# A two-layer trunk kernel: the first loads in two transfers, the third block's load behind the first cast, the last norm weight ahead of the factor

## The chip, the cores and the metric

The kernel runs on one core of one Trainium2 chip. The metric is the device time of one execution in microseconds, lower is better. The core has five engines with their own instruction streams: TensorE (PE, matmuls; PEld is its weight load), VectorE (DVE), ScalarE (ACT), GpSimd (POOL) and SyncE (SP), which here only issues transfers. ACT and POOL issue a few transfers too. Data move between DRAM, on-chip memory (128 partitions) and PSUM, where matmuls accumulate.

## What is computed

The reference is a decoder trunk with 256 positions of width 1024, in float32, with two layers. Each layer is an attention, a SwiGLU feed-forward and a gated per-layer input; a root-mean-square norm stands before each of them and at the end.

```python
def reference(x, p, ...):
    h = x
    for i in range(DEPTH):                                 # DEPTH = 2
        u = _rmsnorm(h, attn_norm_g[i])
        if i % N_MIXERS == 0:                              # layer 0: forgetting attention
            proj = u @ fox_w_in[j]                         # 1024 x (3 * 1024 + 16)
            ...
            h = h + _merge_heads(_fox_attention(q, k, v, log_f)) @ fox_w_o[j]
        else:                                              # layer 1: block-sparse attention, position bias
            ...
            h = h + _merge_heads(_moba_attention(q, k, v, rel_bias_table)) @ moba_w_o[j]
        u = _rmsnorm(h, ffn_norm_g[i])
        gu = u @ ffn_w_in[i]                               # 1024 x 5632
        h = h + (jax.nn.silu(gu[..., :D_FF]) * gu[..., D_FF:]) @ ffn_w_out[i]
        gate = jax.nn.sigmoid(_rmsnorm(h, ple_norm_g[i]) @ ple_w_gate[i])
        h = h + gate * (p[i] @ ple_w_up[i])
    return _rmsnorm(h, final_norm_g)
```

## The kernel before

**Three products for one.** Each float32 operand is split into a rounded part and a remainder (`hi`, `lo`), and each product is the sum of three matmuls (`mm3`, L94 to L96): hi by hi, hi by lo, lo by hi. So each weight tile is fetched from DRAM into a `raw` tile (128 x 1024, 512 KB, six buffers), rounded by ScalarE into `whi` (L169, for some tiles L139 or L187) and subtracted by VectorE into `wlo` (L171, L142, L188). 216 such tiles go through in the order of use. SP issues the fetches one after another (L154, L138, L186). A fetch waits until VectorE has freed its buffer, and everything behind it on SP waits with it. Each transfer also takes the next of eight completion semaphores in turn and waits until the transfer eight before it has landed.

**The start.** TensorE first runs `WARM` = 8 matmuls on constants (L114, tile `cold`). The first product is v = norm(x) by the value weights. x comes transposed, in eight blocks of 128 x 256, and goes with the weight row of the same number. ScalarE scales a block by the norm's gains into `g` (`Norm.block`, L207), VectorE makes its remainder (L209). Block 0 and the gains come in tile `gx`, its weights in `raw` by halves: one half of the weights and the second half of x on SP, the gains with the first half of x and the other half of the weights on ACT. Blocks 1 and 2 come with their weight rows from the array `wx` into tile `hw` (L151), block 1 in two transfers, block 2 in one. Then come the weights of block 3, the rest of x (L295), constants (`con`, L302) and more weight tiles. The first half of each of the first three casts is VectorE's (L162), the others are ScalarE's.

**Order.** A scheduler sets the order of each engine's instructions. `tc.issue_after(x)` keeps what is issued inside it behind x on x's engine. `state["row"]` is set at every fetch of L154 and names the latest.

**The position bias of layer 1.** In layer 0, after the third pair of heads, a table is computed and written to DRAM (`d`, L429). Four transfers spread it from DRAM to DRAM (`d_0` to `d_3`, L434, 768 KB each); they are called in the feed-forward of layer 0, behind the weight fetch of that moment (L816, L817). Layer 1 loads the spread bias (L440).

**Turned probabilities.** The attention of layer 0 turns its probabilities through DRAM: POOL writes `dt` (L655) and reads it back as `pt` (L659), in part also from SP; TensorE takes `pt` in L674 and L676 (`po`).

**The end.** The last layer's gate goes token by token in two halves of 128 tokens. For the last 128 tokens and the last 512 columns, `part` takes 256 columns at a time: a sigmoid (L913), two VectorE steps (L914, L916) and a sum of squares (L959). POOL makes the norm factor from it (L962, `colf`). Then ScalarE scales the first 512 columns (L988), and VectorE scales the last two pieces of 256 by the factor and the norm weight `gb` in one step (L991). `rows` stores each piece (L966).

Of the kernel before, what the change touches and what calls it, by code (L numbers as in the profile page):

```python
# [30 lines left out]
ALU = mybir.AluOpType  # L31

P = 128
# [15 lines left out]
NCHUNK = 54  # L49
WARM = 8  # L50
RAW = 6
# [18 lines left out]

GX = 64 + S
CON = 9 * LINE
# [3 lines left out]
def trunk(ctx: ExitStack, tc: tile.TileContext, xg, wx, xr, pt, w, cst, gf, rel, hot, rvm, out):  # L76
# [47 lines left out]
    hx = [gx[:, GX - S:], hw[:, 0, 0:S], hw[:, 1, 0:S]] + [hr[:, k] for k in range(KT - 3)]  # L124

    state = {"next": 0}

    def half(at=0, entry=0):


        i = state["next"]
        state["next"] += 1
        if i not in (1, 2):
            raw = work.tile([P, HW + LINE], F32, tag="raw", bufs=RAW, name=f"raw{i}")
        ht, lt = (work.tile([P, HW + 2 * LINE], F32R, tag=n, bufs=6, name=f"{n}{i}") for n in ("whi", "wlo"))
        hi, lo = ht[:, at:at + HW], lt[:, at:at + HW]
        if entry:
            nc.sync.dma_start(raw[:, 0:HW], w[i - 2][:, 0:HW])  # L138
            nc.scalar.activation(hi, raw[:, 0:HW], AF.Copy)  # L139
            ats = [(at + FURTHER, 0, entry), (at + LINE, entry, HW)]  # L140
            for a, c0, c1 in ats:
                nc.vector.tensor_tensor(lt[:, a + c0:a + c1], raw[:, c0:c1], f32(hi[:, c0:c1]), op=ALU.subtract)  # L142
            return hi, [lt[:, a + k * P:a + (k + 1) * P] for a, c0, c1 in ats for k in range(c0 // P, c1 // P)]
        if i in (1, 2):
            raw = hw[:, i - 1, S:]
        parts = 2 if i < 2 else 1
        cs = [slice(q * HW // parts, (q + 1) * HW // parts) for q in range(parts)]
        for c in cs:
            if i in (1, 2):
                at = slice(c.start + (S if c.start else 0), c.stop + S)  # L150
                nc.sync.dma_start(hw[:, i - 1, at], wx[i - 1][:, at])  # L151
            else:
                queue = nc.scalar if i == 0 and c.start else nc.sync
                state["row"] = queue.dma_start(raw[:, c], w[max(i - 2, 0)][:, c])  # L154
# [5 lines left out]
        for c in cs:  # L160
            if i < 3 and c.start == 0:
                nc.vector.tensor_copy(hi[:, c], raw[:, c])  # L162
                with tc.issue_after(state["hi0"].ins) if i else nullcontext():
                    got, low = nm.block(i, hx[i], 1 if i else 2)
            elif i == 0:
                with tc.issue_after(got.ins):
                    state["hi0"] = nc.scalar.activation(hi[:, c], raw[:, c], AF.Copy)
            else:
                state["hi"] = state[f"hi{i}"] = nc.scalar.activation(hi[:, c], raw[:, c], AF.Copy)  # L169
            with tc.issue_after(low.ins) if i == 0 else nullcontext():  # L170
                nc.vector.tensor_tensor(lo[:, c], raw[:, c], f32(hi[:, c]), op=ALU.subtract)  # L171
        return hi, lo
# [6 lines left out]
    def gapped(first=0):  # L179
# [5 lines left out]
        ht, lt = (work.tile([P, HW + 2 * LINE], F32R, tag=n, bufs=6, name=f"{n}{i}")[:, at] for n in ("whi", "wlo"))  # L185
        nc.sync.dma_start(raw[:, 0:WW], w[i - 2])  # L186
        nc.scalar.activation(ht, raw[:, 0:WW], AF.Copy)  # L187
# [677 lines left out]
    def ple(layer, nm, ut, nx):  # L865
# [88 lines left out]
        def part(i, bk):  # L954
            c0 = HC + i * S
            first = gate(bk, 1, c0, c0 + S)
            sq = work.tile([P, HC], F32, tag="t2k", bufs=3, name=f"sql{i}")
            hc = summed(1, c0, c0 + S)
            nc.vector.tensor_tensor_reduce(sq[:, 0:S].rearrange("p (m x) -> p m x", m=4), hc, hc, 1.0 / D, ms[:, 1, i:i + 1], op0=ALU.mult, op1=ALU.add,  # L959
                                           accum_out=ms[:, 1, i + 1:i + 2])  # L960
            if i == 1:
                nc.gpsimd.tensor_tensor(col[:, 1:2], ms[:, 1, 2:3], nhalf[:, 0:1], op=ALU.pow)  # L962
            return first
# [19 lines left out]
        for c0 in (0, HC):  # L983
# [3 lines left out]
            rows(0, c0, c0 + HC, nc.sync)  # L987
        nc.scalar.activation(ys[:, 1, 0:HC], ys[:, 1, 0:HC], AF.Copy, scale=col[:, 1:2])  # L988
        rows(1, 0, HC, nc.scalar)
        for c in (slice(HC, HC + S), slice(HC + S, D)):  # L990
            nc.vector.scalar_tensor_tensor(ys[:, 1, c], ys[:, 1, c], col[:, 1:2], gb[:, c], op0=ALU.mult, op1=ALU.mult)  # L991
            rows(1, c.start, c.stop, nc.sync)

# [134 lines left out]
```

## Time and profile before

| | |
|---|---|
| time, median of 3 runs | 634.96 us (634.74 to 635.93) |
| the profiled execution, its own time | 634.63 us |
| its span in the profile | 632.8 us |
| PE busy | 624.2 us, 99% |
| PEld busy | 602.8 us, 95% |
| DVE busy | 467.7 us, 74% |
| ACT busy | 384.7 us, 61% |
| POOL busy | 43.4 us, 7% |
| moved | 135.27 MB, 214 GB/s over the span |

The profile is that of one execution; the span runs from its first instruction to its last. A row of the timeline has the start, the length, the engine, the line of the kernel, the operation, out<-in, the shape and the number of instructions merged, and in brackets the idle time before it with what ended it. A row of issued transfers has the number, the size of one and the median us from its issue to its landing. SPq, ACTq and POOLq are the issues of transfers on an engine. Buffer numbers are left out of names. A sum over the whole span says little about either end of it.

### The profile page before, as it was taken

The numbers are of one execution on the slowest core, as the hardware profiler recorded it, in microseconds if no ns is written. First come the engines' busy times: TensorE is split into PE (matmuls) and PEld (weight loads), VectorE is DVE, ScalarE is ACT, GpSimd is POOL, SyncE is SP. The second block draws the span as 40 slices with busy tenths as digits, with TensorE's granted clock in tenths as the row PEclk, the third lists the DMA queues.
The fourth block names the chain that finished last, engine by engine and source line by source line (L and its number), as shares of the span: only waits on it lengthen the run. The fifth ranks groups of instructions, "written<-read, shape, count | busy, mean of one in ns | idle before, by whom it ended". The sixth has DMA issues, their size and how long they took to land.

```text
span 632.8 us, 13104 instructions
## 1 busy us (share of the span) xinstructions
PE 624.2 (99%) x5241; PEld 602.8 (95%) x5241; DVE 467.7 (74%) x757; ACT 384.7 (61%) x663; POOL 43.4 (7%) x85
## 2 busy tenths in 40 slices
PE   9999999999999999999999999999999999999995
PEld 6899989999999999999989998999999999999984
DVE  6888888886666666668894898979666666666695
ACT  6668887754444445448774798768444444454653
POOL 0103340000000000000000044100000000000001
PEclk9999999999999999999999999999999999999998
DMA  8767878398766666666574698855766666665622
GB/s 336 259 192 236 252 241 314 120 351 259 244 206 197 199 193 208 193 208 180 191 239 171 205 295 232 296 197 180 256 199 186 195 197 202 200 208 180 197 50 85
DMA packets 41885, 135.27 MB, mean 214 GB/s; under 512 B 5248, under 2 KB 10848, under 8 KB 41824
## 3 DMA queue, kind: packets, MB, share of 16 engines
q1 hardware_dynamic: 37616, 124.11, 60.8%
q0 software_dynamic: 3488, 9.44, 5.1%
q10 hardware_dynamic: 720, 0.89, 0.4%
q8 instruction: 41, 0.67, 0.4%
q14 instruction: 20, 0.16, 0.1%
HBM read 126.01 MB, written 8.15 MB: 212 GB/s over the span
## 4 chain that ended last, share of the span: by engine, by line
PE 92%; DVE 3%; DMA 1%; issue 1%; SPq 1%; ACT 0%; POOL 0%; POOLq 0%; DVEq 0%; ACTq 0%
PE gu L95 13%; PE gu L94 13%; PE gu L96 13%; PE fo L96 6%; PE fo L95 6%; PE fo L94 6%; PE pq L94 5%; PE pq L96 5%; PE pq L95 4%; PE wo L94 2%; PE wo L95 2%; PE wo L96 2%; PE v L94 2%; PE v L95 2%; PE v L96 2%; PE v L456 1%
## 5 line engine op out<-in xcount | busy, mean ns | idle before, releaser
L171 DVE TENSOR_TENSOR wlo<-raw,whi 128x1024 fp32r<-128x1024 f32 (+1 forms) x168 | 203.5, 1216 | 65.1 <-ACT whi L169 64.8
L169 ACT ACTIVATE whi<-raw 128x1024 fp32r<-128x1024 f32 x166 | 173.7, 1056 | 94.4 <-issue 42.5
L95 PE MATMUL gu<-g,whi 128*128 128x256 f32 x704 | 194.7, 277 | 0.0
L94 PE MATMUL gu<-g,whi 128*128 128x256 f32 x704 | 194.6, 276 | 0.0
L96 PE MATMUL gu<-g,wlo 128*128 128x256 f32 x704 | 194.5, 276 | 0.0
L96 PEld LDWEIGHTS gu<-g,wlo 128*128 128x128 f32 x704 | 132.3, 188 | 0.0
L95 PEld LDWEIGHTS gu<-g,whi 128*128 128x128 f32 x704 | 132.2, 188 | 0.1
L94 PEld LDWEIGHTS gu<-g,whi 128*128 128x128 f32 x704 | 132.2, 188 | 0.0
L96 PE MATMUL fo<-fp,wlo 128*128 128x256 f32 x352 | 97.3, 276 | 0.0
L95 PE MATMUL fo<-fp,whi 128*128 128x256 f32 x352 | 97.2, 276 | 0.0
L94 PE MATMUL fo<-fp,whi 128*128 128x256 f32 x352 | 97.2, 276 | 0.0
L94 PE MATMUL pq<-g,whi 128*128 128x256 f32 x256 | 71.5, 279 | 0.0
L96 PE MATMUL pq<-g,wlo 128*128 128x256 f32 x256 | 70.9, 277 | 0.1
L95 PE MATMUL pq<-g,whi 128*128 128x256 f32 x256 | 70.8, 277 | 0.0
L188 DVE TENSOR_TENSOR wlo<-raw,whi 128x1080 fp32r<-128x1080 f32 x36 | 46.1, 1282 | 29.9 <-ACT whi L187 29.9
L94 PEld LDWEIGHTS fo<-fp,whi 128*128 128x128 f32 x352 | 66.1, 188 | 0.0
L95 PEld LDWEIGHTS fo<-fp,whi 128*128 128x128 f32 x352 | 66.1, 188 | 0.0
L96 PEld LDWEIGHTS fo<-fp,wlo 128*128 128x128 f32 x352 | 66.1, 188 | 0.0
L187 ACT ACTIVATE whi<-raw 128x1080 fp32r<-128x1080 f32 x36 | 39.6, 1101 | 28.6 <-PE gu L95 27.1
L94 PEld LDWEIGHTS pq<-g,whi 128*128 128x128 f32 x256 | 48.1, 188 | 1.0 <-issue 0.3
L96 PEld LDWEIGHTS pq<-g,wlo 128*128 128x128 f32 x256 | 48.2, 188 | 0.3 <-DVE wlo L171 0.3
L95 PEld LDWEIGHTS pq<-g,whi 128*128 128x128 f32 x256 | 48.1, 188 | 0.1
(194 smaller groups left out, 1038.8 us busy)
## 6 DMA issues: line engine op xcount, KB each, us to landing
raw<-w SPq DMA_DIRECT2D x177, 512.0 KB, 4.4
raw<-w SPq DMA_DIRECT2D x36, 540.0 KB, 4.3
dt<-turn POOLq DMA_DIRECT2D x10, 384.0 KB, 3.4
pt<-dt POOLq DMA_DIRECT2D x40, 96.0 KB, 5.2
d<-d SPq DMA_DIRECT2D x4, 768.0 KB, 7.1
bias<-d SPq DMA_DIRECT2D x4, 512.0 KB, 7.7
pt<-turn POOLq DMA_DIRECT2D x16, 96.0 KB, 3.1
pt<-turn SPq DMA_DIRECT2D x8, 96.0 KB, 3.3
```

The lines of the kernel that those rows point to most:

```text
L94: mm(o, ah, bh, start=start, stop=False, skip_group_check=True)
L95: mm(o, ah, bl, start=False, stop=False, skip_group_check=True)
L96: return mm(o, al, bh, start=False, stop=stop, skip_group_check=True)
L169: state["hi"] = state[f"hi{i}"] = nc.scalar.activation(hi[:, c], raw[:, c], AF.Copy)
L171: nc.vector.tensor_tensor(lo[:, c], raw[:, c], f32(hi[:, c]), op=ALU.subtract)
L187: nc.scalar.activation(ht, raw[:, 0:WW], AF.Copy)
L188: state["lo"] = nc.vector.tensor_tensor(lt, raw[:, 0:WW], f32(ht), op=ALU.subtract)
L456: got = mm(bks[2 * t + hf], x[a][:, t * P:(t + 1) * P], w[b][:, hf * HC:(hf + 1) * HC], start=k + a + b == 0, stop=k + b == KT, skip_group ...
```

## The change

Block 0 now comes whole in tile `gx`, which is widened by 1024 columns: first half of the weights, 64 columns of gains, x, second half of the weights. Two transfers on SP bring it (L121, L122), cut in the middle of x; ACT issues none. Behind the first cast VectorE copies one element per partition into the tile that block 2's transfer writes (L162), so that this transfer waits for the cast, and what stands behind it on SP waits too. `WARM` is 7. `state["row"]` is set once, at the second of the two transfers; the four spreading transfers of the bias name it still.

At the end, `part` multiplies its 256 columns by the norm weight after the sum of squares. The last step only scales: ScalarE 384 columns, VectorE 2 x 320.

```diff
-WARM = 8
+WARM = 7
...
-GX = 64 + S
+GX = 64 + S + HW
...
-    nc.scalar.dma_start(gx[:, 0:GX - P], xg[:, 0:GX - P])
-    gn = gx[:, 0:7 * KT].rearrange("p (n k) -> p n k", k=KT)
+    sides = gx[:, 0:HC], gx[:, GX - HC:]
+    nc.sync.dma_start(gx[:, 0:HC + 64 + P], xg[:, 0:HC + 64 + P])
+    state = {"next": 0, "row": nc.sync.dma_start(gx[:, HC + 64 + P:], xg[:, HC + 64 + P:])}
+    gn = gx[:, HC:HC + 7 * KT].rearrange("p (n k) -> p n k", k=KT)
...
-                queue = nc.scalar if i == 0 and c.start else nc.sync
-                state["row"] = queue.dma_start(raw[:, c], w[max(i - 2, 0)][:, c])
-                if i + c.start == 0:
-                    nc.sync.dma_start(gx[:, GX - P:], xg[:, GX - P:])
+            elif i:
+                nc.sync.dma_start(raw[:, c], w[i - 3][:, c])
...
-                nc.vector.tensor_copy(hi[:, c], raw[:, c])
+                nc.vector.tensor_copy(hi[:, c], part)
+                if i == 0:
+                    nc.vector.tensor_copy(hw[:, 1, 0:1], gx[:, 0:1])
...
+            gc = gb[:, HC:].rearrange("p (m a x) -> p m (a x)", m=4, x=32)[:, :, i * 2 * 32:(i + 1) * 2 * 32]
+            nc.vector.tensor_tensor(hc, hc, gc, op=ALU.mult)
             if i == 1:
                 nc.gpsimd.tensor_tensor(col[:, 1:2], ms[:, 1, 2:3], nhalf[:, 0:1], op=ALU.pow)
...
-        nc.scalar.activation(ys[:, 1, 0:HC], ys[:, 1, 0:HC], AF.Copy, scale=col[:, 1:2])
-        rows(1, 0, HC, nc.scalar)
-        for c in (slice(HC, HC + S), slice(HC + S, D)):
-            nc.vector.scalar_tensor_tensor(ys[:, 1, c], ys[:, 1, c], col[:, 1:2], gb[:, c], op0=ALU.mult, op1=ALU.mult)
-            rows(1, c.start, c.stop, nc.sync)
+        cut = 3 * P
+        nc.scalar.activation(ys[:, 1, 0:cut], ys[:, 1, 0:cut], AF.Copy, scale=col[:, 1:2])
+        rows(1, 0, cut, nc.scalar)
+        for c0, c1 in ((cut, 704), (704, D)):
+            nc.vector.tensor_scalar(ys[:, 1, c0:c1], ys[:, 1, c0:c1], col[:, 1:2], None, op0=ALU.mult)
+            rows(1, c0, c1, nc.sync)
```

The lines that build the arrays on the host follow the new layout and are left out.

Three places in the order of instructions. First SP at the program's start, before the change; the brackets name the engines and transfer semaphores (DMAHW) that a row waits for.

```order
L154 DMA raw_87<-w 128x512
L156 DMA gx<-xg 128x128
L151 DMA hw<-wx 128x768
L151 DMA hw<-wx 128x512
L151 DMA hw<-wx 128x1280
L154 DMA raw_119<-w 128x1024
L295 DMA hw<-xr 128x1280 [waits DMAHW0_49]
L302 DMA con<-cst 128x576 [waits DMAHW1_49]
```

SP at the same place after the change:

```order
L121 DMA gx<-xg 128x704
L122 DMA gx<-xg 128x640
L151 DMA hw<-wx 128x768
L151 DMA hw<-wx 128x512
L151 DMA hw<-wx 128x1280 [waits DVE_49]
L153 DMA raw_116<-w 128x1024
L295 DMA hw<-xr 128x1280
L302 DMA con<-cst 128x576
```

The first two rows carry what four transfers on two queues carried, the fifth waits for VectorE, and the seventh and eighth no longer wait for an earlier landing.

Second, SP in the attention of layer 0, from the transfer that writes the table of the position bias (`d`) on; before the change:

```order
L429 DMA d_518<-rv 16x384 [waits DVE_49]
L154 DMA raw_845<-w 128x1024 [waits DMAHW6_49,DVE_49]
L186 DMA raw_999<-w 128x1080 [waits DMAHW7_49,DVE_49]
L154 DMA raw_1030<-w 128x1024 [waits DMAHW0_49,DVE_49]
L154 DMA raw_1096<-w 128x1024 [waits DMAHW1_49,DVE_49]
L154 DMA raw_1114<-w 128x1024 [waits DMAHW2_49,DVE_49]
```

The same stretch after the change:

```order
L429 DMA d_515<-rv 16x384 [waits DVE_49]
L153 DMA raw_842<-w 128x1024 [waits DMAHW4_49,DVE_49]
L434 DMA d_0_517<-d_515 128x1536 [waits DMAHW2_49]
L186 DMA raw_996<-w 128x1080 [waits DMAHW5_49,DVE_49]
L153 DMA raw_1027<-w 128x1024 [waits DMAHW6_49,DVE_49]
L434 DMA d_1_518<-d_515 128x1536 [waits DMAHW7_49]
L434 DMA d_2_519<-d_515 128x1536 [waits DMAHW0_49]
L153 DMA raw_1093<-w 128x1024 [waits DMAHW1_49,DVE_49]
L434 DMA d_3_520<-d_515 128x1536
L153 DMA raw_1111<-w 128x1024 [waits DMAHW3_49,DVE_49]
```

The four spreading transfers stood 32 rows and more behind the table's write, seven rows apart; now all four follow within eight rows of it.

Third, VectorE at the program's end, before (ISA is the sum of squares with its read-out) and after:

```order
L914 TENSOR_TENSOR pgt_1_768_7966<-pgt_1_768_7966,ut_7585 128x256 [waits Activation_49]
L916 TENSOR_TENSOR end<-ut_7585,pgt_1_768_7966 128x4x64 [waits DVE_49]
L959 ISA sql_7970,msf<-end,msf 128x256 [waits DVE_49]
L959 ISA msf 128x1
L991 SCALAR_TENSOR_TENSOR end<-end,colf 128x256 [waits Pool_49]
L991 SCALAR_TENSOR_TENSOR end<-end,colf 128x256
```

```order
L914 TENSOR_TENSOR pgt_1_768_7964<-pgt_1_768_7964,ut_7582 128x256 [waits Activation_49]
L916 TENSOR_TENSOR end<-ut_7582,pgt_1_768_7964 128x4x64 [waits DVE_49]
L959 ISA sql_7968,msf<-end,msf 128x256 [waits DVE_49]
L959 ISA msf 128x1
L962 TENSOR_TENSOR end<-end 128x4x64 [waits DVE_49]
L994 TENSOR_SCALAR end<-end,colf 128x320 [waits DVE_49,Pool_49]
L994 TENSOR_SCALAR end<-end,colf 128x320
```

The multiply by the norm weight (L962) now stands ahead of the wait for POOL's factor.

More of the change, by code (lines that the diff above doesn't have):

```diff
@@ L119, in trunk @@
     gx = one.tile([P, GX], F32, name="gx")
-    nc.scalar.dma_start(gx[:, 0:GX - P], xg[:, 0:GX - P])
-    gn = gx[:, 0:7 * KT].rearrange("p (n k) -> p n k", k=KT)
+    sides = gx[:, 0:HC], gx[:, GX - HC:]
+    nc.sync.dma_start(gx[:, 0:HC + 64 + P], xg[:, 0:HC + 64 + P])
+    state = {"next": 0, "row": nc.sync.dma_start(gx[:, HC + 64 + P:], xg[:, HC + 64 + P:])}
+    gn = gx[:, HC:HC + 7 * KT].rearrange("p (n k) -> p n k", k=KT)
     hw = work.tile([P, 3, S + HW], F32, tag="bias", bufs=1, name="hw")
     hr = hw[:, 2].rearrange("p (k s) -> p k s", s=S)
-    hx = [gx[:, GX - S:], hw[:, 0, 0:S], hw[:, 1, 0:S]] + [hr[:, k] for k in range(KT - 3)]
-    state = {"next": 0}
+    hx = [gx[:, HC + 64:HC + 64 + S], hw[:, 0, 0:S], hw[:, 1, 0:S]] + [hr[:, k] for k in range(KT - 3)]
     def half(at=0, entry=0):
@@ L132, in half @@
         state["next"] += 1
-        if i not in (1, 2):
+        if i > 2:
             raw = work.tile([P, HW + LINE], F32, tag="raw", bufs=RAW, name=f"raw{i}")
@@ L137, in half @@
         if entry:
-            nc.sync.dma_start(raw[:, 0:HW], w[i - 2][:, 0:HW])
+            nc.sync.dma_start(raw[:, 0:HW], w[i - 3][:, 0:HW])
             nc.scalar.activation(hi, raw[:, 0:HW], AF.Copy)
@@ L159, in half @@
                 table(AF.Abs_reciprocal_sqrt)
-        for c in cs:
+        for q, c in enumerate(cs):
+            part = raw[:, c] if i else sides[q]
             if i < 3 and c.start == 0:
-                nc.vector.tensor_copy(hi[:, c], raw[:, c])
+                nc.vector.tensor_copy(hi[:, c], part)
+                if i == 0:
+                    nc.vector.tensor_copy(hw[:, 1, 0:1], gx[:, 0:1])
                 with tc.issue_after(state["hi0"].ins) if i else nullcontext():
@@ L166, in half @@
                 with tc.issue_after(got.ins):
-                    state["hi0"] = nc.scalar.activation(hi[:, c], raw[:, c], AF.Copy)
+                    state["hi0"] = nc.scalar.activation(hi[:, c], part, AF.Copy)
             else:
-                state["hi"] = state[f"hi{i}"] = nc.scalar.activation(hi[:, c], raw[:, c], AF.Copy)
+                state["hi"] = state[f"hi{i}"] = nc.scalar.activation(hi[:, c], part, AF.Copy)
             with tc.issue_after(low.ins) if i == 0 else nullcontext():
-                nc.vector.tensor_tensor(lo[:, c], raw[:, c], f32(hi[:, c]), op=ALU.subtract)
+                nc.vector.tensor_tensor(lo[:, c], part, f32(hi[:, c]), op=ALU.subtract)
         return hi, lo
@@ L1107 @@
     ins = {
[L1108 removed]
+        "xg": np.concatenate([seq[0][:, :HC], np.pad(gains.reshape(P, 7 * KT), ((0, 0), (0, 64 - 7 * KT))), xt[0], seq[0][:, HC:]], axis=1),
         "wx": wx,
```

8 lines of the change are left out of this document (3 added, 5 removed).

## The prediction

> **What bounds the kernel now.** I read the page first, then the chain of work that ended last over its first 18 us, then the timeline of that stretch, the transfers issued in it, the timeline of the last 8 us, and last the transfers between 40 and 80 us.
>
> ```profile
> span 632.8 us, 13104 instructions
> PE 92%; DVE 3%; DMA 1%; issue 1%; SPq 1%; ACT 0%; POOL 0%; POOLq 0%; DVEq 0%; ACTq 0%
> ...
> 1.65 5.73 DMA hw<-wx
> ...
> 7.97 8.52 PE v L456 x36
> ```
>
> The first two rows are the page's: TensorE (PE) is 92% of a chain of 632.8 us. The last two stand near the head of that chain: a transfer issued at 1.65 that takes 5.73 us, and from 7.97 on nothing but matmuls. So the middle of the kernel costs what its matmuls cost, and this change removes no matmul of the computation. What it can win lies ahead of 7.97 and behind the last matmul, some 7 us at each end. What it can lose may lie anywhere a transfer comes late.
>
> ```profile
> 0.78 3.45 PE L114 MATMUL cold<-const-float32-0.0 128*128 128x512 f32 x8 [0.78 <-PEq L1120]
> 3.80 0.43 DVE L162 CAST whi<-raw 128x512 fp32r<-128x512 f32 x1 [3.80 <-DMA raw<-w]
> 3.98 0.78 ACT L207 ACTIVATE g<-gx 128x128 fp32r<-128x128 f32 x2 [0.81 <-DMA gx<-xg]
> 4.43 2.28 PE L456 MATMUL v<-whi,g 128*128 128x512 f32 x8 [0.20 <-ACT g L207]
> 4.74 0.63 ACT L167 ACTIVATE whi<-raw 128x512 fp32r<-128x512 f32 x1
> 6.55 1.09 PE L456 MATMUL v<-wlo,g 128*128 128x512 f32 x4
> 7.97 2.17 PE L456 MATMUL v<-whi,g 128*128 128x512 f32 x8 [0.33 <-ACT g L207]
> 9.57 0.51 ACT L207 ACTIVATE g<-hw,gx 128x256 fp32r<-128x256 f32 x1 [0.91 <-DMA hw<-wx]
> 10.82 1.07 ACT L169 ACTIVATE whi<-raw 128x1024 fp32r<-128x1024 f32 x1 [0.74 <-DMA raw<-w]
> ```
>
> Here (start, length, then the idle time before it and who ended it) the reader is to see four arrivals: first weights 3.80, gains and x 3.98, block 1 at 7.40 (its matmuls follow at 7.97 after 0.33 us of idle TensorE), block 2 at 9.57 and the weights of block 3 at 10.82. The last two found ScalarE waiting, so they have no slack.
>
> **The start: two transfers, one queue.** Before, four transfers bring block 0: 256 KB of weights and 64 KB of x on SP, 96 KB and 256 KB on ACT, 672 KB in all. After, the same bytes come in two transfers on SP, 352 KB and 320 KB. The first holds half the weights, the gains and half of x. When the old first half landed at 3.80, the 96 KB beside it had landed by 3.98, again 352 KB, so I put the new first landing at 3.80, between 3.4 and 4.0. ScalarE's first scaling then starts with the cast instead of 0.18 us behind it, and the first matmul moves from 4.43 to about 4.25. The second transfer brings what ScalarE used at 4.37 (second half of x, 3.98 and half of 0.78) and 4.74 (second half of weights). I put it at 4.5. The scaling then runs first, about 0.37 us, and the cast at about 4.87 rather than 4.74. So block 0 starts earlier and its second half a little later: its end stays near 7.64 (6.55 + 1.09), at best half of the 0.18 us earlier.
>
> The added 128x1 copy stands on VectorE behind the first cast, ahead of the first subtraction. It is not in the trace; its bounds are nothing and the 0.43 us of the 512-wide cast, and with one column I take it near the lower, 0.1. The cast ends at 4.23 and ScalarE's first scaling, which the subtraction needs, at 4.37 now: VectorE waits there, and that hides it.
>
> The wait: block 2's transfer (L151) now waits on SP for that copy, about 4.3 us. Behind it in the same queue stand the weights of block 3, the rest of x, the constants and four more weight tiles.
>
> ```profile
> hw<-wx SPq DMA_DIRECT2D x1, 384.0 KB, 5.7
> hw<-wx SPq DMA_DIRECT2D x1, 640.0 KB, 7.0
> ...
> 4.00:7.00 3.00, 2.80 (x12) 1.98 (x11) 2.14 (x5) 1.37 (x3) 0.00 (x0) 1.00 0.99 327
> 7.00:10.00 3.00, 2.67 (x12) 1.74 (x11) 2.48 (x5) 1.57 (x3) 0.00 (x0) 1.00 1.01 405
> ```
>
> The first two rows are block 1's x with half its weights, and block 2: size, us from issue to landing. The last two are windows; their last two columns are the DMA engines' busy share and GB/s. Ahead of block 1's data stood 1056 KB, itself included. At 327 to 405 GB/s that is 2.6 to 3.2 us, yet it took 5.73 us from its issue and only the seventh microsecond brought it. So some part of it lagged, with later transfers moving beside it. Held back, only 1312 KB (352, 320, 384, 256) can be in flight before 4.3. I put block 1's landing at 6.4; it needs to be there by 6.9 to remove the idle 0.33 us. If nothing of the lag goes, the gain here is 0; if all of it goes, block 1 follows block 0 at once.
>
> Does the hold starve anything? Of the 3.05 us that the first 352 KB took from issue (0.75) to landing (3.80), 0.9 is moving at 390 GB/s; with half of the rest ahead of the bytes, by estimate they move from 1.8 on, and 1312 KB last until 5.2. Block 2's first bytes follow its issue by the same 1.1 us, at 5.4, so the queue hardly runs dry. The bytes up to block 2 (1952 KB) and block 3 (2464 KB) are the same as before; I take their landings to move ahead by as much as block 1's start needs, 0.4 us, with ends of 0 and 1.5.
>
> Start: 0.33 + 0.09 = **-0.4 us** (ends 0 and -1.0). One dummy matmul less (3.45/8 = 0.43 us) costs nothing by itself: the dummies now end at 3.8, ahead of 4.25.
>
> **The end.** Rows of the last 3 us:
>
> ```profile
> 626.67 0.43 DVE L916 TENSOR_TENSOR end<-ut,pgt 128x256 f32<-128x256 f32 x1
> 626.81 2.79 SPq L966 DMA_DIRECT2D out<-end  x4
> 627.70 0.55 POOL L962 TENSOR_TENSOR colf<-msf,nhalf 128x1 f32<-128x1 f32 x1 [2.94 <-DVE msf L959]
> 628.28 0.72 ACT L988 ACTIVATE end<-end,colf 128x512 f32<-128x512 f32 x1 [0.89 <-POOL colf L962]
> 628.28 0.88 DVE L991 SCALAR_TENSOR_TENSOR end<-end,colf 128x256 f32<-128x256 f32 x2 [0.66 <-POOL colf L962]
> 629.03 0.36 ACTq L966 DMA_DIRECT2D out<-end  x1
> ```
>
> After: two multiplies by the norm weight (128x256) go ahead of the factor. One like it takes 0.43 us (first row); the last one falls into the 0.66 us that VectorE waits for POOL's factor, the first into the wait for the last gate, so both are hidden with 0.2 us to spare. Then VectorE only scales, 2 x 320 columns. That form is not in the rows; a one-input step, the cast, takes 0.43 us for 512, and the old pair took 0.44 apiece for 256, so one lies between 0.27 and 0.55; nearest the cast I take 0.33. The pair ends at 628.94 instead of 629.16. ScalarE's 384 columns instead of 512 take about 0.58 instead of 0.72. SP needs about 0.4 us per issue, so its last issue ends near 629.45 instead of 629.60 (626.81 + 2.79). **-0.15 us** (ends +0.2, if multiply and factor hinder each other, and -0.3).
>
> **What moves besides.** In layer 0's feed-forward, four transfers that spread the position bias from DRAM to DRAM (L434, 768 KB each) were placed behind `state["row"]`, the latest weight fetch. After the change that name stays at the second starting transfer. SP's order now has them right behind the transfer they read, amid the attention of layer 0.
>
> ```profile
> 43.26 0.33 SPq L154 DMA_DIRECT2D raw<-w  x1
> 44.86 0.33 SPq L186 DMA_DIRECT2D raw<-w  x1
> 48.22 8.08 SPq L154 DMA_DIRECT2D raw<-w  x3
> ...
> 124.06 0.56 SPq L434 DMA_DIRECT2D d<-d  x1
> ...
> DMA packets 343, 1.52 MB, mean 370 GB/s; under 512 B 37, under 2 KB 37, under 8 KB 343
> ...
> 44.00:48.00 4.00, 4.00 (x38) 4.00 (x37) 4.00 (x18) 3.03 (x14) 0.00 (x0) 1.00 0.85 255
> 48.00:52.00 4.00, 4.00 (x37) 4.00 (x37) 2.49 (x8) 4.00 (x14) 0.00 (x0) 1.00 0.48 149
> 52.00:56.00 4.00, 4.00 (x45) 3.74 (x44) 4.00 (x7) 3.00 (x4) 1.89 (x4) 1.00 0.58 198
> 56.00:60.00 4.00, 4.00 (x38) 4.00 (x37) 4.00 (x19) 3.39 (x12) 3.79 (x7) 1.00 0.99 318
> ```
>
> By their neighbours in SP's order the first goes out between 43.26 and 44.86, the next two behind 48.22 and the last ahead of 55.97 (the last issue of the x3), not at 124 and later. While the first of them moved (126.4 to 130.5) the engines gave 370 GB/s, so one costs 0.786 MB/370 = 2.1 us of all engines, four 8.5 us. Between 44 and 56 the engines stand idle 0.6 + 2.1 + 1.7 = 4.4 us; the other 4.1 us push later traffic back.
>
> ```profile
> raw<-w SPq DMA_DIRECT2D x1, 512.0 KB, 5.5
> 68.08 1.99 ACT L169 ACTIVATE whi<-raw 128x1024 fp32r<-128x1024 f32 x2
> ...
> 55.41 4.39 POOL L659 DMA_DIRECT2D pt<-dt  x8 [1.58 <-DMA dt<-turn]
> pt<-dt POOLq DMA_DIRECT2D x1, 96.0 KB, 6.3
> L674 PE MATMUL po<-pt,v x8: 379/379/430, 68.3 to 69.3; 128*64 128x256 f32 x8
> ...
> 68.87 4.38 POOL L659 DMA_DIRECT2D pt<-dt  x8 [2.24 <-DMA dt<-turn]
> pt<-dt POOLq DMA_DIRECT2D x1, 96.0 KB, 6.0
> L674 PE MATMUL po<-pt,v x8: 379/379/430, 79.9 to 80.8; 128*64 128x256 f32 x8
> ```
>
> The tightest weight tile is issued at 55.97, lands 5.5 us later at 61.5 and is cast second of the pair, at 69.0: 7.5 us of cover against 4.1. The turned probabilities (pt, read back on POOL's queue): the last is issued 0.55 us before 59.80, lands 6.3 us later at 65.5, and TensorE takes them from 68.3: 2.8 us of cover. The next group, by the last three rows in the same way, lands at 78.7 and is taken from 79.9: 1.2 us of cover. Served strictly in turn behind the spreads they would come 4.1 us late, 1.3 us too late. But in the rows they land in 6.3 us although weight tiles were issued in the queue beside them, in engines busy 99%. I take 1 us of delay, hidden: **0** (ends 0 and +2.9, 4.1 less 1.2).
>
> The Trainium skill, "DMA: Bandwidth & Descriptors", section "Queues, rings and completion order", says that each engine takes turns between the queues it has work for, packet by packet. By that rule a longer SP queue costs POOL's reads little more than a turn each, and this term is 0; by one line for all, it is +1.3. The 6.3 us above agree with turns; no run here shows it with a spread beside them.
>
> **Sum.** -0.4 - 0.15 + 0 = -0.55 us on the profiled execution's 634.63 us (span 632.8, 1.8 around it): 634.1. The median of the runs, 634.96, lies 0.33 higher, so I predict **634.4**.
>
> **Rivals.**
> A. All of the lag goes: block 0's 12 matmuls run at one per 8.52/36 = 0.237 us from 4.2 to 7.05 and block 1 follows, 0.92 us earlier, with the tail -0.2: 633.8. For it: fewer bytes in flight. Against: weights and x of block 0 still arrive as two parts, the second at 4.5.
> B. The start stays: whatever delays one part of a transfer delays it again, and blocks 2 and 3 land at 9.57 and 10.82 as now. Then TensorE wins at 7.97 but waits before block 3. Only the tail stays: 634.8. For it: the same bytes in the same order.
> C, slower. The spreads delay the turned probabilities beyond 2.8 us at 68.3, or beyond the next group's 1.2 us near 80: TensorE stands 1.3 to 2.9 us, 635.7 to 637.3. It decides from 2.8 us of delay on. For it: the engines are 99% busy from 56 on; against: the turns.
> D, slower. The dummies run at 0.43 us each, real matmuls of that width at 0.237, so the array begins at about half speed. One dummy less leaves 0.4 us of idle at 3.8. If full speed then comes some 3 us later, 7 matmuls are done where 13 were, 1.4 us: 635.8. Against: from 4.43 on the real matmuls took 0.28 us each, waits among them, so full speed was there by the end of the eighth dummy at the latest. The Trainium skill, "TensorE: Matmul & The Clock Gate", section "Part 1: The HAM clock gate (the "warmup" mystery)", says the clock is freed after about 3.4 us of activity in a window that runs free of the kernel; seven dummies are 3.0 us, so by it D is possible, and the trace cannot exclude it.
>
> **How the numbers follow.** Forecast 0.50; A 0.17, B 0.15, C 0.12, D 0.06. About 0.2%, 1.27 us, is what a measurement of this kernel can tell from no change: 633.7 to 636.2. Forecast and B lie within; of A a third may reach below it, and some 0.05 for gains I don't see; of C about half and of D a third lie above. Faster 0.10, same 0.82, slower 0.08. The range for 8 in 10 takes in A's and B's times and the lower edge of C: 633.5 to 636.0.
>
> **What would show it.** Right: block 1's matmuls near 7.5 with no idle ahead of them, spreads at 44 to 55 us with no wait of po, VectorE's last pair under 0.7 us. Wrong: ScalarE waiting at 9.57 and 10.82 as before (B), idle before po at 68 or 80 (C), matmuls of block 0 at 0.43 us (D).

## The result, and the profile after

The changed kernel takes **642.05 us** (median of 6 runs, 639.76 to 642.34) against 634.83 us for the kernel before in the same comparison: ratio 1.0103, interval 1.0086 to 1.012. It is slower, by some 6.5 us by the ratio (7.2 by the medians), where 634.4 was predicted. The profiled execution took 642.14 us, its span 640.3, that is 7.5 longer than the kernel before's.

The page of the changed kernel, its first line and two rows of the 40 slices (16 us each; a digit is tenths):

```profile
span 640.3 us, 13103 instructions
...
PE   8999799999999999999999999999999999999995
...
PEclk9999799999999999999999999999999999999998
```

One slice stands out, the fifth, 64 to 80 us: TensorE is busy less than eight tenths of it, and its granted clock drops there too. In the kernel before the clock's row reads:

```profile
PEclk9999999999999999999999999999999999999998
```

The timeline of TensorE in that slice (start, length, idle time before it and what ended it):

```profile
69.28 0.40 PE L592 MATMUL sp<-qkh,qkl 64*128 64x256 f32 x4
71.77 0.65 PE L674 MATMUL po<-pt,v 128*64 128x256 f32 x4 [2.10 <-DMA pt<-dt]
72.22 0.55 PE L676 MATMUL po<-pt,v 128*64 128x128 f32 x4
74.10 1.12 PE L674 MATMUL po<-pt,v 128*64 128x256 f32 x4 [1.33 <-DMA pt<-dt]
```

`po` waits twice for the turned probabilities. Measured from one matmul's start to the next (2.37 us and 1.74 where 0.11 is usual) these waits take 3.9 us. Behind them, windows of 2 us (busy PE, PEld, DVE, ACT, POOL with instructions; then the granted clock, the transfer engines' share, GB/s):

```profile
72.00:74.00 2.00, 0.77 (x8) 0.35 (x4) 1.31 (x10) 0.93 (x4) 0.00 (x0) 0.59 1.03 393
74.00:76.00 2.00, 1.90 (x10) 1.27 (x11) 0.00 (x0) 0.31 (x1) 0.01 (x1) 0.50 0.99 406
76.00:78.00 2.00, 2.00 (x11) 2.00 (x11) 1.33 (x6) 2.00 (x10) 2.00 (x4) 0.50 0.64 232
78.00:80.00 2.00, 2.00 (x14) 2.00 (x14) 0.18 (x1) 2.00 (x9) 2.00 (x5) 0.70 0.74 206
80.00:82.00 2.00, 2.00 (x19) 2.00 (x18) 0.00 (x0) 0.30 (x1) 0.36 (x1) 1.00 0.56 148
```

The clock is 0.50 and TensorE gets through 11 matmuls in 2 us instead of 19. PE reads as fully busy there: a loss of this kind shows in the clock and the count, not in the busy time. From 67.9 to 85.8 us this stage took 6.3 us longer than before: 3.9 of waits and about 2.4 of half clock. Where does pt come late? POOL's timeline, first of the kernel before, then of the changed one (the third row is the eight reads of pt; its bracket is POOL's wait for dt, the write ahead of them):

```profile
52.36 0.74 POOL L655 DMA_DIRECT2D dt<-turn  x1 [18.39 <-DVE turn L644]
53.27 0.55 POOL L655 DMA_DIRECT2D dt<-turn  x1 [0.17 <-issue]
55.41 4.39 POOL L659 DMA_DIRECT2D pt<-dt  x8 [1.58 <-DMA dt<-turn]
```

```profile
53.63 0.74 POOL L655 DMA_DIRECT2D dt<-turn  x1 [18.38 <-DVE turn L644]
54.54 0.55 POOL L655 DMA_DIRECT2D dt<-turn  x1 [0.17 <-issue]
61.14 4.38 POOL L659 DMA_DIRECT2D pt<-dt  x8 [6.05 <-DMA dt<-turn]
```

And the transfers issued from 50 to 64 us (size, median us from issue to landing), before and after:

```profile
dt<-turn POOLq DMA_DIRECT2D x2, 384.0 KB, 3.1
pt<-dt POOLq DMA_DIRECT2D x8, 96.0 KB, 5.8
```

```profile
d<-d SPq DMA_DIRECT2D x3, 768.0 KB, 9.0
...
dt<-turn POOLq DMA_DIRECT2D x2, 384.0 KB, 7.6
pt<-dt POOLq DMA_DIRECT2D x6, 96.0 KB, 8.9
```

(The last two of the eight reads are issued behind 64 us; they took 9 us too.) Both hops are slower, the write by 4.5 us and the read by 3.1. The start shows a third loss:

```profile
7.59 1.98 PE L456 MATMUL v<-whi,g 128*128 128x512 f32 x8
...
10.86 0.69 DVE L160 CAST whi<-hw 128x1024 fp32r<-128x1024 f32 x1 [2.24 <-DMA hw<-wx]
...
11.70 1.63 PE L456 MATMUL v<-whi,g 128*128 128x512 f32 x6 [1.22 <-DVE whi L160]
```

Block 1's matmuls begin at 7.59 without a wait. But the held block 2 landed at 10.84 instead of 9.55, and TensorE stood before its matmuls. Up to 67.9 us the profiled execution is 1.3 us behind the kernel before; the stage from there adds 6.3, and the end wins 0.2.

### The profile page after: what moved, and what is told of

It is laid out like the page before. It is cut to its first block, busy times and chain, and to the rows that moved or that the text cites. A ratio compares the mean times of both kernels' runs of the same rounds, so it can differ in the third digit from the quotient of the medians.

```text
span 640.3 us, 13103 instructions
## 1 busy us (share of the span) xinstructions
PE 627.5 (98%) x5240; PEld 604.9 (94%) x5240; DVE 468.0 (73%) x760; ACT 384.4 (60%) x663; POOL 43.8 (7%) x85
## 4 chain that ended last, share of the span: by engine, by line
PE 87%; DMA 4%; DVE 4%; ACT 1%; issue 1%; POOL 1%; SPq 0%; POOLq 0%; DVEq 0%; ACTq 0%
PE gu L95 13%; PE gu L94 13%; PE gu L96 12%; PE fo L96 6%; PE fo L95 6%; PE fo L94 6%; PE pq L94 4%; PE pq L96 4%; PE pq L95 4%; PE wo L94 2%; PE wo L95 2%; PE wo L96 2%; PE v L94 2%; PE v L95 2%; PE v L96 2%; DMA pt<-dt 1%
## 5 line engine op out<-in xcount | busy, mean ns | idle before, releaser
L171 DVE TENSOR_TENSOR wlo<-raw,whi 128x1024 fp32r<-128x1024 f32 x166 | 202.2, 1223 | 65.4 <-ACT whi L169 65.2
L94 PE MATMUL pq<-g,whi 128*128 128x256 f32 x256 | 72.5, 283 | 0.0
L95 PE MATMUL pq<-g,whi 128*128 128x256 f32 x256 | 71.7, 280 | 0.0
L94 PEld LDWEIGHTS pq<-g,whi 128*128 128x128 f32 x256 | 49.0, 191 | 1.1 <-issue 0.5
L95 PEld LDWEIGHTS pq<-g,whi 128*128 128x128 f32 x256 | 49.0, 191 | 0.1
```

Of the source, the lines that this page charges most:

```text
L94: mm(o, ah, bh, start=start, stop=False, skip_group_check=True)
L95: mm(o, ah, bl, start=False, stop=False, skip_group_check=True)
L171: nc.vector.tensor_tensor(lo[:, c], part, f32(hi[:, c]), op=ALU.subtract)
```

## The experiments

Unless said otherwise each was timed in five rounds beside the kernel before, whose median was 634.3 to 634.5 us.

### The spreads put back

```diff
-                nc.sync.dma_start(raw[:, c], w[i - 3][:, c])
+                state["row"] = nc.sync.dma_start(raw[:, c], w[i - 3][:, c])
```

Against the changed kernel only SP's order differs: the four spreads stand in the feed-forward again.

> The changed kernel with one thing undone: the spreads of the bias go back behind the latest weight fetch (the row name is set again at each fetch), so they issue in the feed-forward as before; the start in two transfers, the held transfer and the new tail stay. Theory 1 (the early spreads cost the middle some 6.3 us: they starve po, and the idle TensorE then runs at half clock): 642.05 - 6.3 = 635.8 us, no idle before po at 68 to 75 us, granted clock 1.00 in every slice; what is left above the kernel before is the start's +1.3 less the tail's 0.2. Rival (the start comes 1.3 us late, which shifts the attention against the weight fetches, and that starves po whatever the spreads do): 640 us or more, po still waits over 2 us.

Measured: 634.46 us (634.29 to 635.68), ratio 1.0003, interval 0.9994 to 1.0012. No wait of `po`, clock 1.00. So nearly the whole loss goes with the order of four transfers that the change did not set out to move. The rival (the late start does it) falls. It came out 1.3 us under my number: most of the start's loss in the profile above is no loss in the median.

### The spreads alone

The kernel before, again with only SP's order different:

```diff
-                    nc.sync.dma_start(gx[:, GX - P:], xg[:, GX - P:])
+                    state["first"] = nc.sync.dma_start(gx[:, GX - P:], xg[:, GX - P:])
...
-                with tc.issue_after(state["row"].ins):
+                with tc.issue_after(state["first"].ins):
```

> The kernel before with one thing done: the four spreads are placed behind the first x transfer instead of the latest weight fetch, so that they issue between 43 and 56 us, as in the changed kernel. Start and tail as before. Theory 1 (the spreads alone starve po and bring the half clock): 634.83 + 6.3 = 641.1 us, between 639.5 and 642.5, with two waits of po of 1.5 to 2.5 us and the granted clock at 0.5 behind them. Rival (it takes the late start as well): within 1 us of 634.8. A third way, the wait of po without the fall of the clock: 637.5 to 639.

Measured: 637.84 us (636.2 to 640.82), ratio 1.0055, interval 1.0035 to 1.0076. The spreads alone do harm, without the late start, but 3.3 us of it by the medians (3.5 by the ratio), not 6.3. Its profiled execution (637.58 us) shows the third way, waits without a fall of the clock:

```profile
68.08 0.65 PE L674 MATMUL po<-pt,v 128*64 128x256 f32 x4 [0.54 <-DMA pt<-dt]
68.53 0.42 PE L676 MATMUL po<-pt,v 128*64 128x128 f32 x4
70.79 0.65 PE L674 MATMUL po<-pt,v 128*64 128x256 f32 x4 [1.84 <-DMA pt<-dt]
```

The one run at 640.82 us has a mean granted clock of 0.991, like the changed kernel's profiled run; the other five have 0.995 to 0.998.

### Without the held transfer

The first experiment's kernel without the one-column copy at L162:

```diff
-                if i == 0:
-                    nc.vector.tensor_copy(hw[:, 1, 0:1], gx[:, 0:1])
```

> The first of these kernels without the one-column copy: block 2's transfer is issued at once, the two large starting transfers and the tail stay, the spreads are in the feed-forward. Theory 1 (the hold is what makes blocks 2 and 3 land 1.3 us late): block 2 lands at 9.5 or earlier, no idle of TensorE near 10 to 11.7, and 1.2 to 1.7 us less than with the copy: 634.1 to 634.6 us. Rival (two large transfers on one queue are what delays the later ones): block 2 still at 10.5 or later, 635.8 us, as with the copy. On block 1: if it was the hold that brought it to 6.36 instead of 7.38, it goes back to 7.2 to 7.4 and TensorE stands 0.2 to 0.4 us before it; if it was the merging, it stays near 6.4.

Measured: 634.3 us (633.67 to 635.46), ratio 0.9998, interval 0.9989 to 1.0007. In its profile block 2 lands at 8.27 and TensorE does not wait: as expected. Block 1 lands at 5.57, so it is not the hold that brings it forward. Against the kernel with the hold the median is only 0.16 us lower, less than a comparison can tell, and not the 1.2 to 1.7 us that I expected.

### The hold alone

```diff
-                nc.vector.tensor_copy(hi[:, c], raw[:, c])
+                nc.vector.tensor_copy(hi[:, c], raw[:, c]); i == 0 and nc.vector.tensor_copy(hw[:, 1, 0:1], raw[:, 0:1])
```

> The kernel before with the hold alone: a copy of one column into block 2's tile behind the first cast, four starting transfers on two queues, tail and spreads as before. Theory 1 (the hold by itself costs about 1.3 to 1.6 us): block 2 lands near 10.8 instead of 9.55, TensorE idle before it, 636.0 us, between 635.7 and 636.5. Rival (the late landings come from the merged transfers): block 2 at 9.6, 634.8 us. Block 1 lands near 6.4 if the hold speeds it, near 7.4 if the merging does.

Measured: 634.67 us (634.15 to 637.21), ratio 1.0006, interval 0.9998 to 1.0015. The expected 636.0 us is refuted. Block 2 landed at 9.54, as early as in the first profile without a hold. So the 1.3 us are not a fixed price: the landings of the start vary from one execution to the next. Over all profiles of this study:

| start | WARM | profiles | block 1's first half lands | block 2 lands | first matmul of the next stage (pq) |
|---|---|---|---|---|---|
| four transfers, no hold | 8 | 3 | 5.77 to 7.38 | 8.98 to 9.55 | 23.06 to 23.63, mean 23.26 |
| two transfers, no hold | 7 or 8 | 3 | 5.57 to 6.51 | 8.27 to 8.89 | 23.04 to 23.14, mean 23.08 |
| four transfers, hold | 8 | 1 | 6.49 | 9.54 | 23.65 |
| two transfers, hold | 7 | 7 | 5.94 to 6.39 | 9.21 to 10.84 | 23.51 to 24.73, mean 23.95 |

In these profiles the hold costs 0.4 to 1.7 us over the two transfers without it, 0.9 in the mean; the medians with and without it show less (0.16 us, or 0.3 by the ratios). The two transfers by themselves bring 0.2 us, and that only against the one profile of before that I argued from, which has the latest block 1 of all fourteen.

### Early spreads, no hold; and the changed kernel again

The changed kernel without the copy, and the changed kernel itself, in one comparison.

> The changed kernel without the one-column copy: the spreads stay early, the two starting transfers and the tail stay. The first four runs left this open: spreads early cost 7.6 us in the changed kernel (642.05 against 634.46 with the row name set again) but only 3.3 us in the kernel before (637.84 against 634.51). Theory A (the held start makes the collision worse, since it lets SP's queue run behind by some 1.3 us): without the hold the spreads cost what they cost in the kernel before, 634.3 + 3.3 = 637.6 us, between 636 and 639, clock 0.995 or higher in most runs. Theory B (the difference lies in the chip or the execution, not in the hold): no less than the changed kernel in the same call, within 0.7 us of it.

> The changed kernel itself, again, beside the others on this chip. Theory A above: 641 to 642.5 us, as in its first runs, clock 0.991 to 0.995. Theory B: near 638 us on a chip on which the kernel before with early spreads takes 638, with a po wait of 2 to 3 us in all and a clock that falls in few runs. Its profile also shows where block 2 lands a second time (10.84 in the first).

Measured: without the hold 639.28 us (636.84 to 640.85), ratio 1.0068, interval 1.0051 to 1.0085; the changed kernel 639.96 us (636.53 to 642.22), ratio 1.0082, interval 1.0061 to 1.0102. The two medians lie within 0.7 us, as theory B has it: there is no sign that the hold makes the collision worse, though the intervals leave room for some 2.5 us. The changed kernel itself met neither number (641 or more, near 638). The changed kernel's own executions differ by up to 6 us, and its profiled one this time (636.53) had one wait of `po` (1.9 us from start to start) and a clock of 0.998; without the hold the profiled one (636.84) had two, 2.0 and 1.4 us from start to start, and 0.998 as well. So the price of the early spreads is a spread of waits, not a constant: against the kernel with the row name set again, by the ratios, 5.0 us here and 6.3 in the first comparison.

### The waits filled with matmuls

```diff
             for n in (0, 2):
+                if layer == 0 and j == 0:
+                    c0 = 128 * n
+                    for _ in range(12 if n else 9):
+                        mm(po[:, c0:2 * S], still.to_broadcast([P, P]), still.to_broadcast([P, 2 * S - c0]), start=True, stop=True, skip_group_check=True)
```

VectorE's and ScalarE's order moves slightly with it: the split of `po` goes behind the last scores of the next heads.

> The changed kernel with matmuls on constants put into the two waits of TensorE before po of the first two heads (9 of 512 columns, 2.1 us, ahead of the first; 12 of 256 columns, 1.4 us, ahead of the second), into the bank that po then overwrites. They fill the idle time and add none as long as the waits are 2.4 and 1.6 us. Theory 1 (the idle time is what lets the clock fall to half): granted clock 1.00 from 70 to 84 us, 0.997 over the span, and the time falls by the half-clock stretch, 6 us at half speed, by 2.5 to 3.1 us under the changed kernel of the same call. Rival (the clock falls for another reason, such as the transfers): clock 0.5 at 74 to 78 as before and the time as the changed kernel's or up to 1 us longer.

> The kernel with the matmuls on constants ahead of po (9 of 512 columns and 12 of 256), with the spreads back in the feed-forward: what the filling costs by itself when nothing is waited for. 9 x 0.237 + 12 x 0.12 = 3.6 us over the kernel without it, 634.46 + 3.6 = 638.0 us. Theory 1 (in the changed kernel the waits are 3 to 4 us and the rest of its loss is the half clock): 637.8 to 638.2, so that with early spreads (639.38) only 1.4 us more is left, waits beyond the filling, and the changed kernel's 639.96 holds more than that. Rival (the filling hides in slack of its own): under 637 us; then the clock's part cannot be read from that pair.

Measured: with early spreads 639.38 us (638.2 to 641.05, 5 runs), ratio 1.0079, interval 1.0066 to 1.0092; with the spreads back in the feed-forward 638.45 us (637.59 to 638.53), ratio 1.0059, interval 1.0045 to 1.0073. The filling costs 3.6 us by the ratios, as worked out, and hides most of the waits: only 1.3 us are left between the two. The clock stayed at 0.996 to 0.998 in all five runs with early spreads. But the time did not fall by 2.5 us under the changed kernel of the same comparison, because there the clock had hardly fallen either (0.995 to 0.998). So this pair agrees with theory 1 and does not settle it.

### Idle time by itself

The kernel before, with TensorE made to wait in the feed-forward, where no `po` and no spread plays a part:

```diff
+            if layer == 0 and fs[0] in (6, 8, 10, 12, 14):
+                mm(bks[fs[0]][:, 0:S], still.to_broadcast([P, P]), prod[fs[0] - 1][0], start=True, stop=True, skip_group_check=True)
...
+                for n in range((f + 5) // 2 if layer == 0 and f in (5, 7, 9, 11, 13) else 0):
+                    nc.gpsimd.tensor_copy(t[:, 0], sg)
+                    nc.gpsimd.tensor_copy(sg, t[:, 0])
```

> The kernel before (start, tail and spreads as they were) with five idle times of TensorE made without any transfer: in the feed-forward of layer 0 the products of five tiles pass through 5, 6, 7, 8 and 9 pairs of copies on POOL, and a matmul on constants ahead of the next tile waits for them. By the 0.29 us of a 128x128 copy a pair takes 0.6 to 1.0 us, so the idle times grow from about 1 to 6 us, one step of 0.6 to 1.0 us at a time. Theory 1 (idle time alone lets the clock fall to half, and it stays there for some 6 us): behind the longer ones, from about 3 to 4 us of idle, the granted clock shows 0.5 and matmuls come every 0.215 us instead of 0.114; behind the shortest not. Rival (the fall at 72 us came from the transfers, not from idle time): 1.00 behind all five, and the time is 634.4 us plus the idle times alone.

Measured in three rounds: 674.61 us (672.19 to 675.34), ratio 1.0635, interval 1.0618 to 1.0653. The idle times came out longer than meant, 2.80, 4.06, 6.36, 6.88 and 7.80 us. The waiting matmul's rows for the first two, then the windows behind each:

```profile
156.73 0.39 PE L783 MATMUL gu<-fp,const-float32-0.0 128*128 128x256 f32 x1 [2.80 <-ACT fp L319]
...
178.54 0.39 PE L783 MATMUL gu<-fp,const-float32-0.0 128*128 128x256 f32 x1 [4.06 <-ACT fp L319]
```

```profile
158.00:160.00 2.00, 2.00 (x20) 2.00 (x19) 0.00 (x0) 0.17 (x1) 0.00 (x0) 1.00 0.01 4
...
178.00:180.00 2.00, 1.46 (x8) 1.46 (x9) 0.43 (x1) 0.42 (x1) 0.04 (x1) 0.72 0.18 72
180.00:182.00 2.00, 2.00 (x11) 2.00 (x11) 0.00 (x0) 0.00 (x0) 0.00 (x0) 0.50 0.00 0
182.00:184.00 2.00, 2.00 (x18) 2.00 (x17) 0.00 (x0) 0.76 (x1) 0.00 (x0) 0.93 0.00 0
```

Behind 2.80 us of idle the clock stays at 1.00, behind 4.06 us it falls to 0.50, and it falls with the three longer ones (6.36, 6.88 and 7.80 us) as well. Weight fetches did move meanwhile, but that does not separate the cases: the transfer engines were 0.77 busy in the 3.4 us ahead of the fall behind 4.06, and 0.70 in the 3.4 us around the end of the idle of 2.80, which brought none. In the kernel before they were 0.99 busy from 56 to 60 us at a clock of 1.00. The profiled span grew by 37.3 us, 9.4 more than the idle times' 27.9, where the rival had the idle times alone. So idle time without any spread is enough, and the rival falls.

### Two spreads early, and two spreads placed behind dt

In the first, the first two spreads stay early and the last two go behind the latest weight fetch. In the second, the two early ones are also held until a named later fetch (the 22nd), behind dt's issue:

```diff
-                with tc.issue_after(state["row"].ins):
+                with tc.issue_after(state["row" if f < 8 else "late"].ins):
```

```diff
-                with tc.issue_after(state["row"].ins):
+                with tc.issue_after(state["row22" if f < 8 else "late"].ins):
```

> The changed kernel with two of the four spreads (the last two) put back into the feed-forward behind the latest weight fetch; the first two stay early. Theory 1 (a sum of transfer time: each spread is 2.1 us of all engines, the idle engine time between 44 and 56 us is 4.4 us): two take 4.2 us, all of it in idle time, so the turned probabilities land as before the change: 634.3 to 635 us, no wait of po. Rival (what hurts is not the total but that a spread stands in the queues while dt is written and read): half the loss or more stays, 637 us or above.

> As the kernel with two early spreads (636.11 us), but these two are placed two and three weight fetches later, so that they issue at about 56 and 59 us, behind the issue of the first group's dt (52.5 to 54 us) instead of ahead of it; the other two stay in the feed-forward. Theory 1 (a transfer of POOL that is issued into saturated engines moves nothing for 4 us instead of 1.4, and the turned probabilities pay that twice, once for dt's write and once for pt's read): now dt of the first group lands 2.8 and 3.4 us after its issue as before, only pt is delayed, within its 2.8 us of cover: 634.5 to 635.3 us. Rival (only the bytes count, two spreads' worth, wherever they stand in this stretch): 636.1 us. A third way: they now meet the second group's dt at 65 us, whose cover is 1.2 us, and po stands near 80 us instead of 68: 635.5 to 637 us with that wait in the profile.

Measured: two early 636.11 us (634.28 to 636.9), ratio 1.0022, interval 1.0012 to 1.0031; two behind dt 635.37 us (634.22 to 637.61), ratio 1.0019, interval 1.0009 to 1.0029. Of the two-early kernel I had expected nothing, since its 4.2 us of transfer time fit into 4.4 us of idle engines. That sum is refuted: there are 1.4 us. The rival's 637 us or more did not come either. By the times alone the two places cannot be told apart, and neither profiled execution (635.17 and 634.54 us, both under their medians) has a wait of `po`, so no trace shows where the slower ones lose it. POOL's rows tell them apart, first with the two early, then with the two behind dt:

```profile
58.68 4.37 POOL L659 DMA_DIRECT2D pt<-dt  x8 [4.78 <-DMA dt<-turn]
```

```profile
55.55 4.38 POOL L659 DMA_DIRECT2D pt<-dt  x8 [1.61 <-DMA dt<-turn]
```

And the second one's transfers between 50 and 64 us:

```profile
dt<-turn POOLq DMA_DIRECT2D x2, 384.0 KB, 3.1
pt<-dt POOLq DMA_DIRECT2D x8, 96.0 KB, 8.0
```

Behind dt's issue the spreads leave dt alone (3.1 us, as before) and slow only the read. Each hop pays for what moves beside it.

### What the runs point to

The kernel with two starting transfers, no hold, the spreads late, the new tail and `WARM` at 8.

> What the runs so far point to: the two large starting transfers and the new tail, no held transfer, the spreads behind the latest weight fetch, and eight matmuls on constants instead of seven. With seven, TensorE stood idle 0.8 to 0.9 us before its first real matmul in every profile of the changed start, and in four of them the first real matmuls then ran at 0.43 us instead of 0.22. Theory (that idle lets the clock fall or delays its rise): idle before the first matmul 0.4 us or less, no run of 0.43 us spacings, and 634.0 to 634.3 us, 0.2 to 0.5 under the kernel before. Rival (block 0 waits for block 1's weights anyway, so the slow matmuls are hidden): 634.3 us, as the kernel without the hold and with seven. A gain over 0.2% (1.3 us) is expected by neither.

Measured: 634.23 us (633.78 to 634.97), ratio 0.9995, interval 0.9986 to 1.0004. It undoes the loss of the changed kernel; against the kernel before no gain can be told. The theory's 634.0 to 634.3 and the rival's 634.3 are met alike, so the run does not choose between them. (The 0.8 to 0.9 us of the expectation run from the start of the last matmul on constants to that of the first real one; the idle time by the profiles is 0.2 to 0.4 us.)

## Why the prediction was wrong

**The spreads: the step that failed.** "I take 1 us of delay, hidden: **0** (ends 0 and +2.9, 4.1 less 1.2)." By the two comparisons the term was worth 5.0 to 6.3 us. The collision was seen, with the place, the cover of 2.8 us and the rival's sign. Two things in its sum were wrong.

First, the delay was laid on one hop. I compared the last read of pt with its use and asked what the spreads do to that read. But a read of pt is issued when dt has landed, and the row that I quoted for it says so in its bracket, "[1.58 <-DMA dt<-turn]". dt's write goes through the same engines: it took 7.6 us instead of 3.1, and the read then 8.9 instead of 5.8. From dt's first issue to the last landing of pt it is 20.4 us instead of 13.1 by the trace. Of these 7.3 us some 3.4 were covered (the second half of the `po` matmuls takes pt only near 69 us), the rest is the 3.9 us that `po` waited. The 4.1 us that I derived as an upper end, spread work minus idle engine time, does not bound it: two spreads, which that sum hides whole, cost 1.4 us.

Second, the price ended at the wait. Rival C counted the time TensorE stands, not that it starts again at half clock. In the profiled execution this adds about 2.4 us. Idle time alone brings it in the idle-time kernel, and among the executions with early spreads some have it (clock 0.991) and some do not (0.998). I had the half clock in view only at the program's start.

The weight I gave to turns between queues was too large. In the 9 us from dt's issue to its landing the trace shows what each queue moved (q1 is SP's, q0 POOL's: packets, MB, share):

```profile
q1 hardware_dynamic: 618, 2.92, 80.6%
q0 software_dynamic: 160, 0.79, 21.1%
```

By the packets, dt's first bytes moved 3.9 us after its issue (1.3 us in the kernel before), and only then did POOL's queue get some 250 of 400 GB/s. The Trainium skill, "DMA: Bandwidth & Descriptors", section "Queues, rings and completion order", gives turns between queues with work; the second part agrees with that, the 2.6 us ahead of it are not in it. They are not a matter of a busy SP queue alone: in the five profiles with four early spreads the first bytes move 3.0 to 3.9 us after the issue, with two early spreads in flight 1.3 us after it. What holds them stays open.

**The hold: "I take their landings to move ahead" failed.** Blocks 2 and 3 were to come 0.4 us earlier, with ends of 0 and 1.5 us earlier; in the profiled execution they came 1.3 us later, outside both ends. Block 2 was issued 1.69 us later and took 6.6 us instead of 7.0 to land: the latency hardly shrank. The queue did not run empty, but it thinned: from 6 to 11 us the engines moved 322 GB/s instead of 402. Why it thinned is open. Over the profiles TensorE comes to the next stage 0.9 us later with the hold.

**The 0.33 us of idle before block 1** that the start was to win was one execution's. Block 1 lands at 6.36 and nothing waits, as forecast. But two other profiles with the old start have it at 6.57 and 5.77, and the two transfers without the hold at 5.57 once, so 6.4 was met without its reason, fewer bytes in flight, being shown. (The 1056 KB of that sum take 2.7 to 3.3 us at its rates, not 2.6 to 3.2.) The first matmul came at 4.33, not at 4.25.

**The dummy: "costs nothing by itself" stays open.** The seven dummies end at 4.1, not 3.8. With seven, five of nine profiles show two to four of the first real matmuls 0.43 us apart instead of 0.23; with eight, none of five, and one has a first gap of 0.59. So the slow beginning of rival D exists, at up to 0.8 us, and partly hides behind block 1. That the eighth dummy prevents it is not shown: five profiles drawn at random from the fourteen would miss all five with eight about once in 16. By the clock records of the traces full clock is granted at 5.7 to 6.7 us in these five profiles and at 3.7 to 5.3 us in the nine others, and in all fourteen it comes at the end of the first stretch of a grid of 3.41 us (last section) in which TensorE is idle for less than 0.5 us. Where that grid lies differs from one execution to the next. That fits the window that the Trainium skill gives in "TensorE: Matmul & The Clock Gate", section "Part 1: The HAM clock gate (the "warmup" mystery)".

**The tail's -0.15 us came out as -0.2, but by luck.** The changed kernel's last rows:

```profile
635.25 0.08 DVE L959 DVE_READ_ACCUMULATOR2_ANT msf<- 128x1 f32 x1
635.37 0.42 DVE L962 TENSOR_TENSOR end<-end 128x256 f32<-128x256 f32 x1
635.42 0.78 POOL L964 TENSOR_TENSOR colf<-msf,nhalf 128x1 f32<-128x1 f32 x1 [2.45 <-DVE msf L959]
636.23 0.61 ACT L991 ACTIVATE end<-end,colf 128x384 f32<-128x384 f32 x1 [1.24 <-POOL colf L964]
636.23 0.68 DVE L994 TENSOR_SCALAR end<-end,colf 128x320 f32<-128x320 f32 x2 [0.43 <-POOL colf L964]
```

From the start of the read-out to the end of the span it is 5.09 us in all ten profiles with the new tail and 5.30 in all four with the old. But the path that I summed became longer: the pair takes 0.68 us (0.66 forecast, 0.88 before), yet POOL's factor takes 0.78 instead of 0.55 beside the multiply, which I had listed as an end. SP's last issue ends 0.14 us later, and the last landing comes 0.16 us later, 4.19 us behind the start of the read-out instead of 4.03. The gain lies behind it. SP ends with a row of nine waits for semaphores, 0.06 us apart where nothing holds them. SP's waits from the last landing on, before (631.57 to 632.1) and after (639.43 to 639.6):

```profile
L1124 SPq EVENT_SEMAPHORE  x7: 28/28/28, 631.6 to 632.0; - x7
```

```profile
L1127 SPq EVENT_SEMAPHORE  x1: 28/28/28, 639.5 to 639.5; - x1
```

Before, the last landing ended the third of the nine waits and six more followed; after the change it ends the ninth. That is 0.37 us less, and the prediction had no such term.

## What to carry to other kernels

A name that a scheduler uses as an anchor ("behind the latest fetch") is part of the order: when an edit stops updating it, find everything that hangs on it. To price a transfer that moves into a busy stretch, follow every hop of the chain that meets it there, each with its own delay, and compare the sum with the cover once. A wait of TensorE can cost more than the wait: 2.1 us of idle in the wrong place brought 6.8 us of half clock behind it. And a stall of 0.3 us in one profile is not yet a stall of the kernel: look at a second execution before counting on it.

## What the runs showed of the hardware

By the clock records of all fourteen traces the granted clock changes only on a grid of 3.41 us, which lies differently in each execution: a half clock lasted 3.41 us once, 6.83 three times and 10.24 once before full clock came back. Cut into the stretches of that grid, the clock fell at the end of every stretch at full clock in which TensorE was idle for 2.09 us or more, and of none in which it was idle for 1.80 or less. Three such stretches (length, busy PE first), the first from the changed kernel, the others from the idle-time kernel:

```profile
68.96:72.37 3.41, 1.31 (x20) 1.05 (x18) 3.41 (x10) 2.79 (x6) 0.56 (x1) 1.00 1.01 313
```

```profile
154.97:158.39 3.42, 1.66 (x14) 1.67 (x15) 0.49 (x2) 0.42 (x1) 1.13 (x3) 1.00 0.70 240
175.45:178.87 3.42, 0.33 (x2) 0.33 (x3) 0.35 (x1) 0.42 (x1) 2.28 (x6) 1.00 0.77 277
```

So in the changed kernel the first wait of `po` alone, 2.10 us in one stretch, brought the fall at 72.37, ahead of the second wait. The longer 2.80 us of the idle-time kernel lay across two stretches, 1.05 and 1.76 us, and brought none; so did the 0.54 and 1.84 us in the kernel with the spreads alone (0.89 and 1.49 us). The Trainium skill, "TensorE: Matmul & The Clock Gate", section "Part 1: The HAM clock gate (the "warmup" mystery)", speaks of an idle window of about 3.4 us. The length agrees with the grid; the stretch with 2.10 us says that such a window need not be empty.

A POOL step on one column takes 0.78 us beside a VectorE multiply of two inputs and 0.54 to 0.55 us without, in every profile here (ten and four). The Trainium skill, "SBUF — State Buffer", section "Who interferes with whom", says that a VectorE instruction with two inputs from that memory contends with a POOL instruction that reads it; these rows agree.
